# Two-operand products of a hybrid backbone moved to DVE, two gate blocks behind phase A's last step, and the modulation's matmuls placed among the attentions' projections

## The chip, the cores and the metric

One core of one Trainium2 chip runs the whole program. The metric is device time in microseconds (us) of one launch, as the median over several runs. Engines are named as in the profile: PE (TensorE matmuls), PEld (PE's weight loads), DVE (VectorE), ACT (ScalarE), POOL (GpSimd), SP (SyncE, which here only issues transfers).

## The reference

Two layers of a hybrid block work on 1024 latent tokens and 256 context tokens of width 1024. Each layer normalises its input with a modulation (shift, scale, gate) computed from a condition vector, projects it, and runs four mixers on columns of the projection: a Hyena long convolution, a bidirectional RWKV-7, a windowed attention and a dense attention with rotary positions. Each mixer's output is multiplied by its SiLU gate; the four are joined and projected back into the residual stream.

```python
def two_sided_fftconv(u, h_fwd, h_bwd, bias):
    L = u.shape[1]
    k = jnp.concatenate([h_fwd, jnp.zeros_like(h_fwd[:1]), h_bwd[:0:-1]], axis=0)
    U = jnp.fft.rfft(u, n=2 * L, axis=1)
    K = jnp.fft.rfft(k, n=2 * L, axis=0)
    y = jnp.fft.irfft(U * K[None], n=2 * L, axis=1)[:, :L]
    return y + u * bias

def hyena_branch(z, ...):
    v, x1, x2 = jnp.split(zc, 3, axis=-1)
    y = x1 * two_sided_fftconv(v, h[:, 0, 0], h[:, 0, 1], bias[0])
    return x2 * two_sided_fftconv(y, h[:, 1, 0], h[:, 1, 1], bias[1])

def rwkv7_scan(...):          # per token, both directions
    sa = jnp.einsum('bhvk,bhk->bhv', S, -kk_t)
    S = S * w_t + sa[..., None] * (kk_t * a_t)[:, :, None, :] + v_t[..., None] * k_t[:, :, None, :]
```

The RWKV state is not stepped token by token in the kernel: each tile of 128 tokens is brought into a form in which a triangular system of 32x32 blocks is solved.

## The kernel before

Matmuls at full precision are made of rounded parts: an operand is split into a high part (`wh`, written by ACT) and the rest (`wl = wr - wh`, L233), and three products are added up: `hhi` with `wh`, `hlo` with `wh`, `hhi` with `wl`. `chan` (L235) does this for a block of 128 projection columns; its output is transposed, so it runs in groups of 512, 512 and (for the context) 256 tokens, each 3 x 8 matmuls into one `acc`. 42 of the 58 blocks go through `chan`, 16 through `attn` (L297), which projects by tiles of 128 tokens.

A layer goes through these stages. Times are those of layer 0 in the profiled execution.

- Normalisation and the first filters of the Hyena (`hy_filters`), up to 133 us.
- `rw` (RWKV's convolutions), the context's filters and the first blocks of `first`, to 267.
- `modulation` (L116 to L152): the shift, scale and gate vectors from the condition. A load `mw` of 128x1024 (512 KB, L127, on SP's queue, three buffers) feeds two matmuls of 512 columns into `mps` (L130). Layer 0 does here its own gate and all of layer 1's: 32 loads, 64 such matmuls (the trace has four records for each load, as each runs in two passes). To 340.
- `attn`: the attentions' projections, with norms and rotary positions; q and k are stored as `qk_d`. To 476.
- Phase A (`phase_a`): ten tiles of 128 tokens go through `stage_a`, which makes the RWKV's decays, keys and the masked products `GG` (L591 to L598); beside it run Hyena's convolutions and the first gate blocks. Then the triangular systems are solved (L630 to L652) in 31 steps of a product `tmp` and a subtraction on `X`; here POOL takes two columns of each step and DVE the others. The last solve ends with a copy `XR` (L651) at 767; the stretch 729 to 774 is called the tail below.
- The Hyena (`hyena`), to 931: transposes `pd` (L1380), a transform of two streams by `pr` matmuls (L1396) and butterflies (`Dft.pair`, `Dft.odd`, `Dft.even`, `Dft.eight`), the product with the filter `Kf` (L1409, L1410, each cut into one half on DVE and one on POOL), the sums L1411 and L1412, and the way back (`pi`, L1441). Four such iterations follow one another in a layer. Its `u` lies in room that the last solve gives back. Beside it run six gate blocks (`beside`, the SiLU gates g = 1, 2, 3 of two blocks each; L274 and L275).
- `phase_b`, the attentions and the output projection, to 1458. Layer 1 follows in the same way to 2657 without a modulation and without context outputs.

The order on each engine is set by a list scheduler which simulates the program and gives each engine its instructions in the order of estimated readiness. Engines then run theirs strictly in that order and wait on semaphores. `nc.any` lets the scheduler choose the engine. `issue_after` (through `k.behind`) ties a matmul behind a given PE instruction; `k.spread` spreads blocks over the marks, which are PE instructions of the stage beside.

Of the kernel before, what the change touches and what calls it, by code (L numbers as in the profile page):

```python
# [170 lines left out]
def norm_in(k, hp, ap):  # L171
# [5 lines left out]
    with ExitStack() as es:  # L177
# [27 lines left out]
        for (t0, n), at, raw in zip(groups, ((hp, "lo8"),) + room, raws):  # L205
            i = 0 if t0 < 8 else 1
            low = lo[t0 * 128] = part(at, n, F32R, "hlo")
            for kc in range(8):
# [7 lines left out]
class Proj:  # L216
# [206 lines left out]
class Rwkv:  # L423
# [1235 lines left out]
```

## Time and profile before

| what | value |
| --- | --- |
| three runs | 2659.18, 2665.2, 2669.92 us; median 2665.2 |
| the profiled execution | 2658.42 us; span 2656.6, the granted clock 0.904 of full |
| PE busy | 2263.1 us (85%) |
| PEld busy | 1855.2 us (70%) |
| DVE busy | 1740.2 us (66%) |
| ACT busy | 1090.8 us (41%) |
| POOL busy | 1021.2 us (38%) |

The span is the time from the first to the last instruction of the profiled execution; 1.8 us lie around it. Busy shares say little about one stage, so the windows view, which cuts the span into stages, is the one to begin with.

### The profile page before, as it was taken

Reading aid. Unit: us, or ns where it says so; the run is one execution under the profiler, and the core shown is the slowest. Engines: PE = TensorE matmul, PEld = TensorE weight load, DVE = VectorE, ACT = ScalarE, POOL = GpSimd, SP = SyncE. Lnnn points to the kernel's source line nnn. Section 1 sums busy time; section 2 is a strip of 40 time slices with the busy share of each in tenths; the row PEclk is TensorE's granted clock in tenths of the full one; section 3 lists DMA queues with packets and bytes.
Section 4 is the critical chain, followed back from the end, with each engine's and each line's share of the span. In section 5 each row is a group of like instructions: output and inputs, shape, how many; then the busy total and the mean of one; then the engine's idle time right before and its main releaser. Section 6 shows DMA issues by size and latency. Waiting matters only on the chain. (4 is left out here: it accounts for less than half of the span.)

```text
span 2656.6 us, 45224 instructions
## 1 busy us (share of the span) xinstructions
PE 2263.1 (85%) x16864; PEld 1855.2 (70%) x16864; DVE 1740.2 (66%) x3710; ACT 1090.8 (41%) x2581; POOL 1021.2 (38%) x1279
## 2 busy tenths in 40 slices
PE   7799599899736779999899898989893586999898
PEld 3688089687636658787677797977672475888666
DVE  5976047578767856557634686657876886656743
ACT  5422023454411047566744322335441104776651
POOL 1632014356656712111432243323655763111342
PEclk9899799898867889999999899989885787999999
DMA  7223743555341354743433322444554226473242
GB/s 255 99 80 109 250 127 108 150 160 164 121 145 60 118 185 130 215 155 99 139 107 111 103 87 107 124 134 134 150 167 145 77 74 187 155 209 120 92 155 98
DMA packets 288695, 359.11 MB, mean 135 GB/s; under 512 B 108007, under 2 KB 229910, under 8 KB 283100
## 3 DMA queue, kind: packets, MB, share of 16 engines
q1 hardware_dynamic: 261704, 261.60, 31.7%
q0 software_dynamic: 11232, 70.78, 7.8%
q10 hardware_dynamic: 15540, 23.84, 2.8%
q8 instruction: 133, 2.18, 0.3%
q14 instruction: 86, 0.70, 0.1%
HBM read 227.31 MB, written 128.84 MB: 134 GB/s over the span
## 5 line engine op out<-in xcount | busy, mean ns | idle before, releaser
L233 POOL TENSOR_TENSOR wl<-wr,wh 128x1024 fp32r<-128x1024 f32 x58 | 149.3, 2579 | 290.0 <-ACT wh L232 243.7
L246 PE MATMUL acc<-hhi,wh 128*128 128x512 f32 (+1 forms) x896 | 221.2, 385 | 13.8 <-ACT wh L232 8.9
L985 DVE TENSOR_REDUCE st<-S 128x1 f32<-128x512 f32 (+1 forms) x320 | 172.6, 558 | 85.1 <-PE S L981 52.0
L246 PE MATMUL acc<-hlo,wh 128*128 128x512 f32 (+1 forms) x896 | 218.8, 378 | 2.6 <-DVE hlo L212 2.6
L246 PE MATMUL acc<-hhi,wl 128*128 128x512 f32 (+1 forms) x896 | 213.3, 375 | 0.0
L995 ACT ACTIVATE P<-S,st 128x512 f32<-128x512 f32 (+1 forms) x320 | 184.6, 587 | 39.8 <-DVE st L988 23.9
L246 PEld LDWEIGHTS acc<-hhi,wh 128*128 128x128 f32 x896 | 159.3, 198 | 45.6 <-ACT wh L232 10.8
L246 PEld LDWEIGHTS acc<-hlo,wh 128*128 128x128 f32 x896 | 157.8, 195 | 32.3 <-issue 4.5
L246 PEld LDWEIGHTS acc<-hhi,wl 128*128 128x128 f32 x896 | 157.9, 195 | 28.2 <-issue 3.0
L1011 PE MATMUL pt<-ident,P 128*128 128x128 f32 x976 | 160.5, 284 | 13.4 <-ACT P L995 7.1
L980 PE MATMUL S<-kp,qs 128*128 128x256 f32 (+2 forms) x384 | 143.4, 381 | 27.0 <-ACT P L995 18.3
L951 ACT COPY PT<-pt 128x512 f32<-128x512 f32 (+2 forms) x265 | 129.0, 506 | 49.1 <-PE pt L1011 46.7
L1011 PEld LDWEIGHTS pt<-ident,P 128*128 128x128 f32 x976 | 111.0, 142 | 44.6 <-issue 12.7
L1021 PE MATMUL O<-PT,V 128*64 128x256 f32 x976 | 138.4, 391 | 3.0 <-ACT PT L951 3.0
L981 PE MATMUL S<-kp,qs 128*128 128x256 f32 (+2 forms) x384 | 121.1, 326 | 3.6 <-DMA kp<-qk_d 3.6
L980 PEld LDWEIGHTS S<-kp,qs 128*128 128x128 f32 x384 | 75.8, 197 | 48.3 <-ACT P L995 28.1
L232 ACT ACTIVATE wh<-wr 128x1024 fp32r<-128x1024 f32 x58 | 60.7, 1057 | 110.7 <-PE acc L246 89.9
L1021 PEld LDWEIGHTS O<-PT,V 128*64 128x64 f32 x976 | 72.5, 138 | 45.1 <-issue 6.7
L337 PE MATMUL acc<-wh,hhi 128*128 128x256 f32 x608 | 93.4, 296 | 2.6 <-ACT wh L232 2.6
L337 PE MATMUL acc<-wl,hhi 128*128 128x256 f32 x608 | 88.5, 287 | 5.0 <-POOL wl L233 5.0
L258 ACT COPY zp<-acc 128x512 f32<-128x512 f32 (+1 forms) x64 | 33.7, 531 | 139.8 <-PE acc L246 80.1
L591 PEld LDWEIGHTS p_g<-AR,BKT 64*128 64x128 f32 x640 | 74.7, 218 | 23.2 <-DVE GG L598 5.5
(402 smaller groups left out, 5944.4 us busy)
## 6 DMA issues: line engine op xcount, KB each, us to landing
IN<-in_d POOLq DMA_DIRECT2D x18, 2048.0 KB, 9.4
wr<-in_w_in POOLq DMA_DIRECT2D x58, 512.0 KB, 4.2
mw<-in_mod_w SPq DMA_DIRECT2D x48, 512.0 KB, 4.6
in_d<-BK SPq DMA_DIRECT2D x20, 512.0 KB, 2.6
in_d<-AL SPq DMA_DIRECT2D x20, 512.0 KB, 2.7
kp<-qk_d SPq DMA_DIRECT2D x32, 320.0 KB, 7.8
qk_d<-qo SPq DMA_DIRECT2D x72, 128.0 KB, 1.9
in_d<-GG SPq DMA_DIRECT2D x18, 512.0 KB, 3.9
```

The source lines that it names most:

```text
L232: w.k.nc.scalar.activation(h, r, AF.Copy)
L233: w.k.nc.gpsimd.tensor_tensor(lw, r, h.bitcast(F32), op=ALU.subtract)
L246: nc.tensor.matmul(ps[:, :n], a[:, kc * 128:(kc + 1) * 128], b[:, kc, t0:t0 + n], start=(i == 0 and kc == 0), stop=(i == 2 and kc == 7))
L337: nc.tensor.matmul(ps[:, :256], x_[:, kc, t * 128:(t + 1) * 128], w_[:, kc, :], start=(n == 0 and kc == 0), stop=(n == 2 and kc == 7))
L591: nc.tensor.matmul(pg[:, hp, c], BKT[q, hp, c], AR[q, :, hp, half(c)], start=True, stop=True)
L951: nc.any.tensor_copy(o, i)
L980: nc.tensor.matmul(ps[:, w0:w0 + w], qs[:, hd % 2, hd // 2], kp[kv][0][:, t0:t0 + w], start=True, stop=False)
L981: nc.tensor.matmul(ps[:, w0:w0 + w], qs[:, hd % 2, hd // 2], kp[kv][1][:, t0:t0 + w], start=False, stop=not masks)
L985: TR(ng[:, i:i + 1], ps[:, :w0], axis=AX.X, op=ALU.max, negate=True)
L995: nc.scalar.activation(P[:, :w], ps[:, :w], AF.Exp, bias=gm, accum_out=den[:, i:i + 1])
L1011: nc.tensor.transpose(pt[:, i, :], P[:, i * 128:(i + 1) * 128], k.ident)
L1021: nc.tensor.matmul(O[kv * 64:kv * 64 + 64, 0], V[:, t, kv * 64:kv * 64 + 64], PTs[kv][:, i], start=(i == 0), stop=(i == nt - 1))
```

## The change

There are three parts.

The first: nearly every operation of POOL on two operands in SBUF goes to DVE. In all, POOL's instructions go from 1284 to 409, DVE's from 3712 to 4148; PE's 12744 and SP's 962 stay. Where DVE and POOL shared a step (the solve's columns, the product with `Kf`) one DVE instruction on the whole width takes its place. Where ACT copied from PSUM and POOL multiplied (`GG` of odd parity, `om` in the attention), one DVE product reads PSUM. Of the 58 splits `wl`, 42 (those of `chan`) go to DVE; the 16 of `attn` stay. Copies of `PV` and `ST` go to `nc.any`.

The second: the two blocks of gate 1 are tied behind the last mark of phase A (`end`), where before all six blocks were spread over the Hyena's matmuls; the other four still are.

The third: the modulation of layer 0 is written after 18 steps of `attn`'s generator instead of ahead of it, with its pool on the other side of SBUF.

The lines below are the diff's core. Left out are the same replacement of `PT` or `nc.gpsimd` by DVE in `operands`, `stage_a` (`ss`, `bs`), `Dft.even`, `Dft.eight`, the filters, the output projection's `wol`, and the context's Hyena.

```diff
-    def split(w, r, h, lw):
+    def split(w, r, h, lw, eng):
         w.k.nc.scalar.activation(h, r, AF.Copy)
-        w.k.nc.gpsimd.tensor_tensor(lw, r, h.bitcast(F32), op=ALU.subtract)
+        eng.tensor_tensor(lw, r, h.bitcast(F32), op=ALU.subtract)
...
-        w.split(r, h, lw)
+        w.split(r, h, lw, nc.vector)
...
-        pace = w.k.spread([x[1] for x in w.GR[-n:]] * len(todo), *part) if part else []
-        w.k.marks = []
+        if isinstance(part, tuple):
+            pace = w.k.spread([x[1] for x in w.GR[-n:]] * len(todo), *part)
+            w.k.marks = []
+        else:
+            pace = [part] * (n * len(todo)) if part else []
...
-                    e = TT
-                    if par:
-                        nc.scalar.activation(o, s, AF.Copy)
-                        s, e = o, PT
-                    e(o, s, gmask[:, d, :z].unsqueeze(1).to_broadcast([128, 4, z, 64]), op=ALU.mult)
+                    TT(o, s, gmask[:, d, :z].unsqueeze(1).to_broadcast([128, 4, z, 64]), op=ALU.mult)
...
-            PC = 2
-            tmp2 = sp.tile([128, 31 * PC], F32, tag="tmp2", bufs=1, name="tmp2")
             for j in range(31):
-                a, q = 31 - j, j + 1
-                c = min(q, PC)
-                for e, m, s, z in ((nc.gpsimd, tmp2, 0, c), (eng, tmp, c, q)):
-                    if z > s:
-                        n = z - s
-                        t = m[:P, 0:a * n].rearrange("p (q a) -> p q a", q=n)
-                        e.tensor_tensor(t, Lx[:P, j:j + 1, j + 1:].to_broadcast([P, n, a]), X[:, s:z, j:j + 1].to_broadcast([P, n, a]), op=ALU.mult)
-                        e.tensor_tensor(X[:, s:z, j + 1:], X[:, s:z, j + 1:], t, op=ALU.add)
+                a, n = 31 - j, j + 1
+                t = tmp[:P, 0:a * n].rearrange("p (q a) -> p q a", q=n)
+                TT(t, Lx[:P, j:j + 1, j + 1:].to_broadcast([P, n, a]), X[:, :n, j:j + 1].to_broadcast([P, n, a]), op=ALU.mult)
+                TT(X[:, :n, j + 1:], X[:, :n, j + 1:], t, op=ALU.add)
...
-        nc.scalar.activation(o, O[:, 1], AF.Copy)
-        nc.gpsimd.tensor_tensor(o, o, gt[:, :, t0:t0 + 128], op=ALU.mult)
+        nc.vector.tensor_tensor(o, O[:, 1], gt[:, :, t0:t0 + 128], op=ALU.mult)
...
-        h = R // 2
-        for a, z, e in ((h, R, TT), (0, h, PT)):
-            s = slice(a, z)
-            e(t[:, s], W[:, s], Kf[:, s, 1:2, :].to_broadcast([p, z - a, 2, 128]), op=ALU.mult)
-            e(W[:, s], W[:, s], Kf[:, s, 0:1, :].to_broadcast([p, z - a, 2, 128]), op=ALU.mult)
-            e(W[:, s, 0], W[:, s, 0], t[:, s, 1], op=ALU.subtract)
-            e(W[:, s, 1], W[:, s, 1], t[:, s, 0], op=ALU.add)
+        TT(t, W, Kf[:, :, 1:2, :].to_broadcast([p, R, 2, 128]), op=ALU.mult)
+        TT(W, W, Kf[:, :, 0:1, :].to_broadcast([p, R, 2, 128]), op=ALU.mult)
+        TT(W[:, :, 0], W[:, :, 0], t[:, :, 1], op=ALU.subtract)
+        TT(W[:, :, 1], W[:, :, 1], t[:, :, 0], op=ALU.add)
...
-                    if not last:
-                        for a, parts in ((l, (1,)), (l + 1, (0, 1))):
-                            with k.pool(f"mod{a}") as rs, k.pool(f"modp{a}", 1, PSUM) as rp:
-                                modulation(k, a, parts, 3, rs, rp)
                     with k.pool(f"pa{l}") as sa, k.pool(f"pap{l}", 1, PSUM) as pq:
-                        run(w.attn(sa, pq))
+                        at = w.attn(sa, pq)
+                        for _ in range(18):
+                            next(at)
+                        if not last:
+                            for a, parts in ((l, (1,)), (l + 1, (0, 1))):
+                                with tc.using_default_side(LEFT), k.pool(f"mod{a}") as rs, k.pool(f"modp{a}", 1, PSUM) as rp:
+                                    modulation(k, a, parts, 3, rs, rp)
+                        run(at)
...
                         run(rw.phase_a(re, rs, rp))
+                    end = k.marks[-1][1]
...
-                    w.beside([(g, i) for g in (1, 2, 3) for i in range(2)], PACE_H)
+                    w.beside([(1, i) for i in range(2)], end)
+                    w.beside([(g, i) for g in (2, 3) for i in range(2)], PACE_H)
```

How the order on the engines moves is shown at three places. First PE around the modulation of layer 0, in the kernel before. `mps` are the modulation's matmuls, `acc<-hhi,wh` those of the convolutions' blocks, `pk` those of the context's filters, and `acc<-wh_2240,hhi` the projections'.

```order
L246 MATMUL acc<-hhi,wl 128x512 x8
L1501 MATMUL pk<-sm,F 128x256 x2
...
L130 MATMUL mps<-mw,scc 2x512 x48
L145 MATMUL mpt<-ident,mr 128x128 x4
L130 MATMUL mps<-mw,scc 2x512 x16
L337 MATMUL acc<-wh_2240,hhi 128x256 x24
L337 MATMUL acc<-wl_2241,hhi 128x256 x8
```

And the same engine after: the end of the filters and the projections' first group, and a later place in the projections.

```order
L130 MATMUL mps<-mw,scc 2x512 x4
L1489 MATMUL pk<-sm,F 128x256 x2
L1489 MATMUL pk<-H,F 128x256 x2
...
L130 MATMUL mps<-mw,scc 2x512 x8
L340 MATMUL acc<-wh_2060,hhi 128x256 x24
L130 MATMUL mps<-mw,scc 2x512 x4
L340 MATMUL acc<-wl_2061,hhi 128x256 x8
...
L313 MATMUL qpt<-ident,qq 128x128
L130 MATMUL mps<-mw,scc 2x512 x6
L340 MATMUL acc<-wh_2468,hhi 128x256 x8
L340 MATMUL acc<-wl_2469,hhi 128x256 x8
```

One block of 64 matmuls, broken only by four transposes, has become pieces of two to eight, from the context's filters into the second half of the projections. Of the 32 loads 14 stand ahead of the second group of tiles of the projections, 18 behind.

Second, PE at the end of phase A in layer 0, before and after. `p_g` and `p_r` are phase A's last products, `pd` and `pr` the Hyena's first.

```order
L591 MATMUL p_g<-AR,BKT 128x128 x16
L620 MATMUL p_r<-VV,GG 64x64 x16
L1380 MATMUL pd<-ident,zc 128x128 x32
L1396 MATMUL pr<-u,F 128x128 x8
L246 MATMUL acc<-hhi,wh 128x512 x2
L1396 MATMUL pr<-u,F 128x128 x8
L246 MATMUL acc<-hhi,wh 128x512 x6
```

```order
L594 MATMUL p_g<-AR,BKT 128x128 x16
L619 MATMUL p_r<-VV,GG 64x64 x16
L246 MATMUL acc<-hhi,wh 128x256 x8
L246 MATMUL acc<-hlo,wh 128x256 x8
L246 MATMUL acc<-hhi,wl 128x256 x8
...
L246 MATMUL acc<-hhi,wl 128x256 x8
L1371 MATMUL pd<-ident,zc 128x128 x32
L1387 MATMUL pr<-u,F 128x128 x4
```

Seven groups of 24 matmuls, three of 256 columns and four of 512, now stand between the last `p_r` and the first `pd`. In layer 1 there are four, all of 512.

Third, DVE in an iteration of the Hyena in layer 0, before and after. `Z<-W,Kf` is the product with the filter, `gt<-gt,acc` a gate block's product.

```order
L1229 SCALAR_TENSOR_TENSOR G<-s_7009,s_6978 128x512
L1230 SCALAR_TENSOR_TENSOR G<-s_7009,s_6978 128x512
L1233 TENSOR_TENSOR W<-G 128x2x2x128
L1234 TENSOR_TENSOR W<-G 128x2x256
L275 SCALAR_TENSOR_TENSOR gt<-gt,acc 128x512
L1409 TENSOR_TENSOR Z<-W,Kf 128x1024
L275 SCALAR_TENSOR_TENSOR gt<-gt,acc 128x256
L1410 TENSOR_TENSOR W<-W,Kf 128x1024
L1411 TENSOR_TENSOR W<-W,Z 128x4x128
L1412 TENSOR_TENSOR W<-W,Z 128x4x128
```

```order
L1214 TENSOR_TENSOR W<-s_6811 128x2x128
L1215 TENSOR_TENSOR W<-s_6811 128x256
L275 SCALAR_TENSOR_TENSOR gt<-gt,acc 128x512
L1224 TENSOR_TENSOR W<-G 128x2x2x128
L1225 TENSOR_TENSOR W<-G 128x2x256
L1397 TENSOR_TENSOR Z<-W,Kf 128x2048
L233 TENSOR_TENSOR wl<-wr,wh 128x1024
L275 SCALAR_TENSOR_TENSOR gt<-gt,acc 128x512
L1398 TENSOR_TENSOR W<-W,Kf 128x2048
L1399 TENSOR_TENSOR W<-W,Z 128x8x128
L1400 TENSOR_TENSOR W<-W,Z 128x8x128
```

The two products and sums have twice their width, `Dft.even`'s operations (L1212 to L1215 after) and a split `wl` stand in DVE's row too.

## Rows read from the trace of the kernel before

**Rows 1.** Windows: busy time (instructions) of each engine by stage; then clock, DMA share, GB/s.

```profile
0.00:133.00 133.00, 95.87 (x463) 64.18 (x464) 104.48 (x144) 60.88 (x103) 55.93 (x55) 0.90 0.52 177
...
266.60:339.60 73.00, 41.18 (x133) 4.27 (x133) 2.69 (x9) 4.31 (x6) 5.91 (x8) 0.79 0.73 250
339.60:476.00 136.40, 135.28 (x1084) 133.37 (x1083) 81.01 (x314) 42.00 (x110) 44.88 (x36) 0.99 0.37 110
476.00:729.00 253.00, 225.32 (x1499) 182.12 (x1497) 194.29 (x343) 120.18 (x236) 143.17 (x216) 0.86 0.51 151
...
774.40:931.50 157.10, 113.73 (x624) 100.38 (x622) 133.97 (x128) 16.85 (x27) 110.85 (x72) 0.84 0.27 89
...
2059.00:2215.30 156.30, 100.95 (x518) 87.89 (x516) 134.81 (x125) 14.34 (x21) 109.77 (x72) 0.79 0.31 95
```

**Rows 2.** Timeline of PE in the modulation: start, length, instruction, idle before and releaser.

```profile
266.60 2.74 PE L130 MATMUL mps<-mw,scc 128*2 128x512 f32 x12 [0.68 <-ACT sets L1502]
...
311.24 1.03 PE L130 MATMUL mps<-mw,scc 128*2 128x512 f32 x4 [1.36 <-DMA mw<-in_mod_w]
```

**Rows 3.** Timeline of DVE in the Hyena of layer 1.

```profile
2059.15 0.69 DVE L1215 TENSOR_TENSOR s<-s,pr 128x512 f32<-128x512 f32 x1 [6.21 <-PE pr L1396]
2059.75 0.68 DVE L1217 TENSOR_TENSOR s<-s,pr 128x512 f32<-128x512 f32 x1
2060.47 0.42 DVE L1240 TENSOR_TENSOR s<-s 128x256 f32<-128x256 f32 x1
2060.81 0.42 DVE L1241 TENSOR_TENSOR s<-s 128x256 f32<-128x256 f32 x1
...
2062.62 2.81 DVE L1243 TENSOR_TENSOR s<-s 128x512 f32<-128x512 f32 x1
...
2087.99 0.69 DVE L1243 TENSOR_TENSOR s<-s 128x512 f32<-128x512 f32 x1 [1.15 <-POOL s L1417]
...
2095.51 0.69 DVE L1215 TENSOR_TENSOR s<-s,pr 128x512 f32<-128x512 f32 x1 [1.07 <-PE pr L1396]
```

**Rows 4.** Timeline of POOL in the same stretch.

```profile
2062.49 2.40 POOL L1429 TENSOR_TENSOR zc<-zc 128x1024 f32<-128x1024 f32 x1 [10.27 <-DMA zc<-hy_d]
```

**Rows 5.** Groups by line: count | busy us, mean ns of one | idle before.

```profile
L1409 DVE TENSOR_TENSOR Z<-W,Kf 128x1024 f32<-128x1024 f32 x8 | 25.4, 3178 | 0.2
```

**Rows 6.** Timeline of DVE in the first filters.

```profile
74.38 1.23 DVE L1321 TENSOR_TENSOR sm<-H 128x1024 f32<-128x1024 f32 x1
75.53 2.75 DVE L210 TENSOR_SCALAR raw<-raw,gs,sh 128x256 f32<-128x256 f32 x2
```

**Rows 7.** Timeline of PE at the tail and the beginning of the Hyena, layer 0.

```profile
727.85 0.91 PE L620 MATMUL p_r<-VV,GG 64*64 64x64 f32 x12 [2.93 <-POOL GG L598]
...
768.02 3.68 PE L1380 MATMUL pd<-ident,zc 128*128 128x128 f32 x16 [15.79 <-ACT u L1381]
...
779.63 1.98 PE L246 MATMUL acc<-hhi,wl 128*128 128x512 f32 x8
781.44 1.12 PE L246 MATMUL acc<-hhi,wh 128*128 128x256 f32 x8
782.39 1.12 PE L246 MATMUL acc<-hlo,wh 128*128 128x256 f32 x8
```

**Rows 8.** Timeline of DVE, the end of the last solve, layer 0.

```profile
766.25 0.68 DVE L651 COPY XR<-X 32x1024 f32<-32x1024 f32 x1 [1.34 <-POOL X L649]
```

**Rows 9.** Groups by line: the mask product of `GG`.

```profile
L598 POOL TENSOR_TENSOR GG<-GG,gmask 128x512 f32<-128x512 f32 x36 | 48.2, 1341 | 12.2 <-ACT GG L596 12.1
...
L598 DVE TENSOR_TENSOR GG<-p_g,gmask 128x512 f32<-128x512 f32 x36 | 24.6, 684 | 14.1 <-PE p_g L591 14.1
```

**Rows 10.** The page's groups, and who waited for PE's `acc` (us, times).

```profile
L233 POOL TENSOR_TENSOR wl<-wr,wh 128x1024 fp32r<-128x1024 f32 x58 | 149.3, 2579 | 290.0 <-ACT wh L232 243.7
...
L232 ACT ACTIVATE wh<-wr 128x1024 fp32r<-128x1024 f32 x58 | 60.7, 1057 | 110.7 <-PE acc L246 89.9
...
  ACT wh L232: 89.9, 28
```

More of the change, by code (lines that the diff above doesn't have):

```diff
@@ L328, in attn @@
                     r3 = r.rearrange("p (k c) -> p k c", k=8)
-                    w.split(r3, wh[:, :, b * 128:(b + 1) * 128], wl[:, :, b * 128:(b + 1) * 128])
+                    w.split(r3, wh[:, :, b * 128:(b + 1) * 128], wl[:, :, b * 128:(b + 1) * 128], nc.gpsimd)
                 H = 4 if half == 0 else 2
@@ L510, in stage_a @@
             nc.any.tensor_copy(ss[0], sig)
-            PT(ss[1], sig, ss[0].bitcast(F32), op=ALU.subtract)
+            TT(ss[1], sig, ss[0].bitcast(F32), op=ALU.subtract)
             E = []
@@ L560, in stage_a @@
                 bs = w1("bs")
-                PT(bs, kd[:, 0, :], kd[:, 1, :], op=ALU.add)
-                PT(bs, bs, r_, op=ALU.mult)
-                PT(bs, bs, rv[:, 2, :], op=ALU.mult)
+                TT(bs, kd[:, 0, :], kd[:, 1, :], op=ALU.add)
+                TT(bs, bs, r_, op=ALU.mult)
+                TT(bs, bs, rv[:, 2, :], op=ALU.mult)
                 nc.vector.tensor_reduce(w.bon[:, b, :], h4(bs), axis=AX.X, op=ALU.add)
@@ L725, in stage_b @@
                 for c in range(2):
-                    nc.gpsimd.tensor_copy(pv[half(1 - c), c], VS[half(1 - c)].rearrange("p (h v) -> p h v", h=4))
+                    nc.any.tensor_copy(pv[half(1 - c), c], VS[half(1 - c)].rearrange("p (h v) -> p h v", h=4))
                 PV.append(pv)
             if need_y:
-                nc.gpsimd.tensor_copy(ST[:, 1792:2048], VV[:, 0, :])
+                nc.any.tensor_copy(ST[:, 1792:2048], VV[:, 0, :])
             cols = lambda x: x.rearrange("p a (h e) -> p h a e", h=4)
@@ L1220, in even @@
         o = out.rearrange("p s j e -> p (s j) e")
-        s.PT(out[:, 0], AB[:, 0], AB[:, 1], op=ALU.add)
-        s.PT(out[:, 1], AB[:, 0], AB[:, 1], op=ALU.subtract)
-        s.PT(o[:, 4:8:3], A1, B1[:, ::-1], op=ALU.add)
-        s.PT(o[:, 5:7], A1[:, ::-1], B1, op=ALU.subtract)
+        s.TT(out[:, 0], AB[:, 0], AB[:, 1], op=ALU.add)
+        s.TT(out[:, 1], AB[:, 0], AB[:, 1], op=ALU.subtract)
+        s.TT(o[:, 4:8:3], A1, B1[:, ::-1], op=ALU.add)
+        s.TT(o[:, 5:7], A1[:, ::-1], B1, op=ALU.subtract)
     def odd(s, out, TU, CD):
@@ L1243, in eight @@
         s.TT(AB, S[:, 0::2], S[:, 1::2], op=ALU.add)
-        s.PT(AB1, S[:, 0::2], S[:, 1::2], op=ALU.subtract)
+        s.TT(AB1, S[:, 0::2], S[:, 1::2], op=ALU.subtract)
         s.even(out, AB, AB1[:, 0], AB1[:, 1])
@@ L1292, in hy_filters @@
     nc, A = k.nc, k.A
-    TT, PT = nc.vector.tensor_tensor, nc.gpsimd.tensor_tensor
+    TT = nc.vector.tensor_tensor
     R, p = R8, 128
@@ L1321, in hy_filters @@
             TT(sm, H[:, 0], H[:, 1], op=ALU.add)
-            PT(H[:, 1], H[:, 0], H[:, 1], op=ALU.subtract)
+            TT(H[:, 1], H[:, 0], H[:, 1], op=ALU.subtract)
             pm = (sm, H[:, 1])
@@ L1361, in hyena @@
     nc, A = k.nc, k.A
-    TT, PT = nc.vector.tensor_tensor, nc.gpsimd.tensor_tensor
+    TT = nc.vector.tensor_tensor
     n, p, R = L, 128, R8
@@ L1416, in forward @@
         TT(D[:, 0:2], W[:, 0:4:2], W[:, 1:4:2], op=ALU.subtract)
-        PT(S[:, 0:2], W[:, 0:4:2], W[:, 1:4:2], op=ALU.add)
-        PT(S[:, 2:4], W[:, 4:6], W[:, 6:8], op=ALU.add)
+        TT(S[:, 0:2], W[:, 0:4:2], W[:, 1:4:2], op=ALU.add)
+        TT(S[:, 2:4], W[:, 4:6], W[:, 6:8], op=ALU.add)
         ft.eight(Z, S, D, True)
@@ L1428, in inverse @@
             nc.sync.dma_start(out=gx[:, 1], in_=zd[:, 2, hf, 0:n])
-            PT(gx[:, 0], gx[:, 0], gx[:, 1], op=ALU.mult)
+            TT(gx[:, 0], gx[:, 0], gx[:, 1], op=ALU.mult)
             gv = gx[:, 0].rearrange("q (t r) -> q r t", r=R)
@@ L1463, in ctx_filters @@
     nc, A = k.nc, k.A
-    TT, PT = nc.vector.tensor_tensor, nc.gpsimd.tensor_tensor
+    TT = nc.vector.tensor_tensor
     bank = lambda nm: pp.tile([128, 512], F32, tag="b", bufs=3, name=nm)
@@ L1490, in ctx_filters @@
         TT(sm, H[:, 0], H[:, 1], op=ALU.add)
-        PT(H[:, 1], H[:, 0], H[:, 1], op=ALU.subtract)
+        TT(H[:, 1], H[:, 0], H[:, 1], op=ALU.subtract)
         pm = (sm, H[:, 1])
@@ L1509, in ctx_hyena @@
     nc, A = k.nc, k.A
-    TT, PT = nc.vector.tensor_tensor, nc.gpsimd.tensor_tensor
+    TT = nc.vector.tensor_tensor
     bank = lambda nm: pp.tile([128, 512], F32, tag="b", bufs=3, name=nm)
@@ L1521, in ctx_hyena @@
     gx = load(tile_("gx", [2, C]), k.gt_d[0:256, L:TOK].rearrange("(h p) t -> p h t", p=128))
-    PT(gx, gx, zc[:, 2], op=ALU.mult)
+    TT(gx, gx, zc[:, 2], op=ALU.mult)
     ux = []
@@ L1543, in ctx_hyena @@
             TT(Z[:, m, 0], Z[:, m, 0], t[:, 1], op=ALU.subtract)
-            PT(Z[:, m, 1], Z[:, m, 1], t[:, 0], op=ALU.add)
+            TT(Z[:, m, 1], Z[:, m, 1], t[:, 0], op=ALU.add)
         mj = [(m, j) for m in range(2) for j in range(2)]
@@ L1574, in program @@
     run = lambda g: [None for _ in g]
-    R = "right"
+    LEFT, R = "left", "right"
     with k.pool("cp", 1) as cp, k.pool("dp", 1, DRAM) as dp:
```

5 lines of the change are left out of this document (2 added, 3 removed).

## The prediction

> **What bounds the kernel now.** I read the busy time by stage first, because the whole-span shares mix stages with different limits. Six of its rows stand in [rows 1]. In the reader's place I would look for stages whose PE column is close to their length, and those whose PE column is not. The attentions' projections keep PE busy for 135.28 us of 136.40: there only PE work counts. Four other stretches leave PE idle.
>
> - The modulation, 73.00 us long: PE has 41.18 us, DVE 2.69, ACT 4.31, POOL 5.91. Nothing but transfers (250 GB/s) and the small matmuls is there. The PE timeline shows how it goes: four records of 1.03 us per load, each after an idle gap that ends with the arrival of `mw` [rows 2].
> - The hyena, 157.10 us in layer 0 and 156.30 in layer 1: DVE 133.97 and 134.81, POOL 110.85 and 109.77, PE 113.73 and 100.95 [rows 1]. DVE and POOL are both near full, and both are slowed: the next view, one iteration on DVE and POOL [rows 3, 4], has the same addition of 128x512 (L1243) at 2.81 us while POOL multiplies `zc`, and at 0.69 us 25 us later.
> - Phase A, 253.00 us in layer 0: PE 225.32 at a granted clock of 0.86, DVE 194.29, POOL 143.17 [rows 1]. No engine is full; the chain through the tiles is the limit.
> - The solve's tail before the hyena: PE stops at 728.8 (727.85 + 0.91) and works on the hyena's second stream only at 768.02 [rows 7].
>
> **The change part by part.**
>
> *The hyena's products on DVE.* The row that matters is the product of 1024 columns: 3178 ns mean on DVE while POOL works on the other half [rows 5]. The same width alone, with POOL quiet, takes 1.23 us, and the next instruction starts after 75.53 − 74.38 = 1.15 [rows 6]. So a half costs 2.6 times its price alone, which is more than one engine needs for both (2.30). The Trainium skill has this on the page "SBUF — State Buffer", section "Who interferes with whom": a DVE operation with two SBUF operands and a GpSimd operation that reads SBUF use one read port, under a lock. The trace agrees by the three rows just named.
>
> The price of a DVE instruction in a row is start to start: 0.60 us for 128x512 (2059.75 − 2059.15) and 0.34 for 128x256 (2060.81 − 2060.47) [rows 3], 1.15 for 128x1024 [rows 6]. A 2048-column one isn't in the trace; two of 1024 bound it from above at 2.30, and the slope (0.55 per 512 columns) gives 2.25, which I take. One iteration (two streams joined, two transforms) then is on DVE alone: 20 of 512 columns = 12.0; 12 of 256 = 4.1; 2 of 1024 = 2.3; 2 of 2048 = 4.5; 2 of 512 for `u` = 1.2. Sum 24.1 us. Add about 2.5 for gate blocks that fall in (a `wl` of 1.15 and two gates of 0.60) and 2 for the turn through PE: 28.5. The iteration before takes 2095.51 − 2059.15 = 36.4 us [rows 3]. Four iterations and 6 us of beginning and end: 120 against 157.1 and 156.3, that is −37 per layer. Bounds: nothing gained, if the chain and not the load is the limit, and at best 24.1 × 4 + 6 = 102, −55.
>
> *The two early gate blocks.* Behind phase A's last step stand seven groups in layer 0, before the transposes `pd`. By the hyena's rows a group of 512 is 3 × 1.83 = 5.5 us (from 779.63 to 781.44 for eight) and one of 256 is 3 × 0.95 = 2.9 [rows 7]: 4 × 5.5 + 3 × 2.9 = 30.7 us on PE. The hole there is 768.02 − 728.76 = 39.3 us. It covers them, with 3.7 for the first `pd` set now behind them, by 5 us. That hides them and takes 31 us of PE from the hyena. On DVE they put a `wl` of 1.15, four gates of 0.60 or less and waits into the last solve, which ended with `XR` at 766.25 [rows 8]; the solve's own steps lose their waits for POOL (1.34 us at the end). I charge 7 us of tail per layer: 3.6 for these instructions, 3.7 for the `pd` set when it ends up last. Bounds 0 and 15. Hyena and tail: −30 per layer, −60 in all; the ends are −110 and +30.
>
> *The modulation amid the projections.* 32 loads of 512 KB took 73.00 us, 2.28 each, of which 1.03 is PE [rows 1, 2]. In the changed order 14 loads are used before the second group of tiles of the projections and 18 later. For the first 14 I take 25 us: between 14.4 (all had arrived) and 32 (all paced by the transfers as before), nearer the upper, since they stand in the convolutions' last rows and there are few matmuls between. The other 18 cost PE 18.5, in a stage where PE is full [rows 1]. 73.0 − 25 − 18.5 = −30. Bounds: 0 if every load is waited for as before, since PE goes in order and a late `mw` stops the projections; −44 if all stands hidden with PE at 0.91 us per load (2.74 us for 12 would be the best run of them). SP, which issues the loads, now holds them between stores of `qk_d`; a full pool makes SP wait there and delays stores, whose readers come only in the attentions.
>
> *Phase A.* POOL's work goes to DVE at about half the price: the mask product of the 128x512 `GG` is 1341 ns on POOL and 684 on DVE, 36 each [rows 9], and ACT's copy ahead of it goes. Each chain becomes shorter: the two waits of `p_r` for `GG` go. But the load grows: 194.29 + 143.17 / 2 = 265.9 us of DVE in 253.00 if nothing of 194.29 was contention. With the products freed (a third of it by the hyena's ratio) it is nearer to 220. I take −10 for both layers; bounds −40 (the 28 us of PE idle in layer 0 gone and part of layer 1's) and +30 (13 us each, and a little).
>
> *Filters, convolutions, output projection, attentions.* At the start DVE has 104.48 of 133.00 and POOL 55.93 [rows 1], so 104.48 + 28 fills the stage without contention relief; elsewhere PE bounds. The 42 moved `wl` splits cost POOL 2579 ns each, and 1.15 on DVE [rows 10, 6]; POOL waited 243.7 us for `wh` ahead of them [rows 10], which was free on POOL and is not on DVE. I take −8; bounds −25 and +25. Attention: the copy on ACT and product on POOL become one DVE product beside PE's work: 0, ±10.
>
> **Sum.** −60 − 30 − 10 − 8 = −108. On the profiled execution, 2658.42 us, that is 2550. The median of the runs shown is 2665.2, 6.8 above it, so 2557 on the runs' scale; I take 2556.
>
> **The rivals.**
>
> *DVE becomes the bound outside the hyena.* What speaks for it is the 265.9 above, and the full start. Then phase A costs +13 per layer, the start +10, and the hyena and modulation still give 30 and 60 less 20 for a hyena bound by its chain: 2665 + 36 − 70 = 2631. Against it is the 3178 ns row: the relief is on DVE too. The Trainium skill's page "Perfetto Trace Analysis", section "Optimizing Scalar/DVE Operations", says that a saturated DVE may be relieved by offloading to Scalar or even GPSIMD, with the warning that the shared port may make this useless: by its first half this rival, by the second the forecast. The trace shows the load in [rows 1] and the lock in [rows 5].
>
> *The modulation gains nothing.* The loads are paced by the transfers wherever they stand, and PE waits in order. Speaks for it: each gap in [rows 2] ends with `mw`. Against: PE has 135.28 us of other matmuls beside them [rows 1]. 2556 + 30 = 2586.
>
> *The split in DVE's queue, the slower side.* ACT writes `wh` after waiting for PE's `acc`: 89.9 us over 28 waits, 3.2 each [rows 10]. The `wl` product stood on POOL, where such a wait held up nobody; on DVE all behind it waits, and PE waits for that. 42 splits × (3.2 + 1.15) = 183 us if all of them stop the critical work. Between none and all, the change turns from gain to loss when 108 / 4.35 = 25 of the 42 do. At 32, the time is 2665 − 108 + 139 = 2696. Against: the scheduler places the splits by its own estimate of their readiness, and the convolutions have slack on DVE (two `wl` buffers).
>
> *The halves were not slowed by each other.* Then the hyena's 2048-column products cost 2 × 3.2 and DVE alone is slower than both: per iteration about 24.1 + 8 = 32, plus turns 36: hyena at 0, and 2556 + 60 = 2616. Against it are rows 5 and 6 together.
>
> **Chances and range.** Forecast (sum within 35 us) 0.55; modulation gains nothing 0.15; DVE bound elsewhere 0.13; halves not slowed by each other 0.05; the split in the queue 0.05; a gain larger than 143 us, all bounds at their good ends, 0.07. What this kernel's measurement can tell from no change is 0.5%, 13 us. The forecast's own range is 2521 to 2591; with the rivals, 2505 to 2630 holds 8 in 10. Faster by over 0.5%: 0.89. Within: 0.05. Slower: 0.06.
>
> **What would show it.** Hyena: the `Z<-W,Kf` product at 128x2048 near 2.3 us, iterations of 28 to 30 us, no POOL in that stage. If that product is above 4 us, the reading of rows 5 and 6 is wrong. Tail: 30 us of `acc` matmuls in the old hole, and `XR` no later. Modulation: no stretch of `mps` alone longer than 30 us; if the projections' stage has idle on PE that ends with `mw`, the second rival is right. Phase A: DVE below 225 us; over 245, with PE idle ending with DVE, the first. Splits: DVE idle that ends with ACT's `wh` over 40 us in sum is the third. Above 2640 the forecast has failed altogether.

## The result, and the profile after

The changed kernel took 2538.16 us (median of 4 runs, 2534.96 to 2539.31), the kernel before 2662.19 beside it. The ratio is 0.9536, 95% interval 0.9498 to 0.9574: faster by 4.6%, 124 us. The forecast was 2556. The profiled execution has a span of 2537.5 us against 2656.6, so 119.1 us have to be found in the two traces.

The page's first lines come first. Read them beside the table of before: DVE's busy time is the same to 1 us (1740.2 before) with 436 more instructions, while POOL's fell from 1021.2 to 270.0.

```profile
PE 2231.6 (88%) x16864; PEld 1844.7 (73%) x16864; DVE 1740.8 (69%) x4146; ACT 1079.7 (43%) x2564; POOL 270.0 (11%) x404
```

The windows of after by stage (columns as in [rows 1]) answer to [rows 1]: the remainder of the modulation's loads ahead of the projections; the projections; phase A; the tail; the Hyena; in layer 1 the Hyena alone.

```profile
243.40:277.40 34.00, 23.52 (x88) 9.65 (x87) 13.85 (x19) 6.20 (x8) 5.89 (x8) 0.85 0.69 245
277.40:429.50 152.10, 151.36 (x1153) 133.29 (x1152) 77.74 (x322) 43.49 (x113) 36.09 (x34) 0.99 0.52 163
429.50:664.40 234.90, 211.77 (x1468) 172.33 (x1466) 194.41 (x410) 106.35 (x209) 14.72 (x28) 0.89 0.56 165
664.40:724.20 59.80, 40.47 (x227) 36.23 (x226) 37.93 (x104) 12.30 (x21) 1.12 (x2) 0.81 0.56 184
724.20:849.10 124.90, 88.86 (x503) 79.93 (x502) 110.83 (x176) 12.17 (x20) 0.00 (x0) 0.84 0.32 97
...
1968.20:2094.60 126.40, 76.90 (x420) 68.52 (x419) 109.36 (x172) 10.41 (x16) 0.00 (x0) 0.78 0.35 99
```

In phase A, DVE is busy for 194.41 us with 67 instructions more than before, where it was 194.29 in a longer stage [rows 1]. In the Hyena POOL does nothing, and DVE's busy time fell from 133.97 to 110.83 although it now does both halves (and 11 gate products where 16 stood). The stages, cut at the same instructions in both traces (last `p_r` of phase A, last `XR`, first and last work of the Hyena, and so on), give this balance, in us:

| stage | before | after | difference | forecast |
| --- | --- | --- | --- | --- |
| start to the projections' end, layer 0 | 471.9 | 428.9 | -43.0 | -38 (modulation -30, and the -8 for all filters and splits) |
| phase A, both layers | 501.5 | 460.5 | -41.0 | -10 |
| last `p_r` to last `XR` | 38.2, 39.4 | 51.6, 43.7 | +13.4, +4.3 | +14 |
| last `XR` to the Hyena's first sum | 7.5, 6.2 | 8.2, 7.2 | +1.7 | - |
| the Hyena | 157.1, 156.3 | 124.9, 126.4 | -32.2, -29.9 | -74 |
| phase_b, attentions, output projection, layer 0 | 527.7 | 533.9 | +6.2 | 0 |
| all else of layer 1 | | | +1.4 | 0 |

DVE in an iteration of the Hyena in layer 0 answers to [rows 3]: `Z<-W,Kf` is now the whole product of 2048 columns, and the additions that had cost 2.81 us beside POOL stand at 0.69.

```profile
752.85 0.69 DVE L1206 TENSOR_TENSOR s<-s,pr 128x512 f32<-128x512 f32 x1 [1.42 <-PE pr L1387]
...
758.52 0.69 DVE L1234 TENSOR_TENSOR s<-s 128x512 f32<-128x512 f32 x1
...
763.92 2.29 DVE L1397 TENSOR_TENSOR Z<-W,Kf 128x2048 f32<-128x2048 f32 x1
...
783.13 0.69 DVE L1206 TENSOR_TENSOR s<-s,pr 128x512 f32<-128x512 f32 x1 [1.86 <-PE pr L1387]
```

The iteration takes 783.13 − 752.85 = 30.3 us. Between these rows DVE idles only for 0.65, 0.50 and 1.86 us, each time for PE's `pi` or `pr`: the Hyena is now bound by DVE.

PE in the modulation answers to [rows 2]. Before the projections' second group of tiles the loads still come in bursts; later, beside two bursts of three, single loads stand 1.7 to 3.5 us apart among the projections, and PE waits for one of them once.

```profile
243.39 2.74 PE L130 MATMUL mps<-mw,scc 128*2 128x512 f32 x12
...
275.58 1.88 PE L130 MATMUL mps<-mw,scc 128*2 128x512 f32 x4 [4.82 <-DMA mw<-in_mod_w]
281.87 1.04 PE L130 MATMUL mps<-mw,scc 128*2 128x512 f32 x8
...
348.97 1.03 PE L130 MATMUL mps<-mw,scc 128*2 128x512 f32 x4
352.02 1.03 PE L130 MATMUL mps<-mw,scc 128*2 128x512 f32 x4
354.36 1.03 PE L130 MATMUL mps<-mw,scc 128*2 128x512 f32 x4
357.81 1.03 PE L130 MATMUL mps<-mw,scc 128*2 128x512 f32 x4 [0.74 <-DMA mw<-in_mod_w]
```

The tail in layer 0 answers to [rows 7, 8]: DVE's copies around the last two solves, then PE.

```profile
677.62 0.69 DVE L644 COPY XR<-X 64x1024 f32<-64x1024 f32 x1
...
689.18 0.68 DVE L634 COPY Lx<-Ld 32x1024 f32<-32x1024 f32 x1 [6.18 <-DMA Ld<-ls_d]
...
715.31 0.68 DVE L644 COPY XR<-X 32x1024 f32<-32x1024 f32 x1
```

```profile
662.36 2.04 PE L619 MATMUL p_r<-VV,GG 64*64 64x64 f32 x32
664.33 2.07 PE L246 MATMUL acc<-hhi,wh 128*128 128x256 f32 x8
...
694.78 1.12 PE L246 MATMUL acc<-hhi,wl 128*128 128x256 f32 x8
695.74 1.96 PE L1371 MATMUL pd<-ident,zc 128*128 128x128 f32 x16
717.03 3.68 PE L1371 MATMUL pd<-ident,zc 128*128 128x128 f32 x16 [19.33 <-ACT u L1372]
```

The gate groups fill the hole from 664.33 to 695.74, 31.4 us. But the solve ahead of the last copies its `XR` only 13.2 us after the last `p_r` (677.62 − 664.40), and the last one waits for it. In the kernel before it was 5.9 us, by its row beside [rows 7], and from there to the copy `Lx` of the last solve 8.3 us against 11.6 now:

```profile
734.64 0.69 DVE L651 COPY XR<-X 64x1024 f32<-64x1024 f32 x1
...
742.96 0.68 DVE L635 COPY Lx<-Ld 32x1024 f32<-32x1024 f32 x1 [7.62 <-DMA Ld<-ls_d]
```

In the changed kernel two products of the early gate groups stand among the last steps of the solve ahead, and DVE waits for ACT before each:

```profile
668.80 0.42 DVE L275 SCALAR_TENSOR_TENSOR gt<-gt,acc 128x256 f32<-128x256 f32 x1 [1.05 <-ACT gt L274]
...
674.48 0.69 DVE L275 SCALAR_TENSOR_TENSOR gt<-gt,acc 128x512 f32<-128x512 f32 x1 [0.71 <-ACT gt L274]
```

In layer 1 the trace has five groups between the last `p_r` and the first `pd` (1917.21 to 1947.00), one more than counted above from the order.

### The profile page after: what moved, and what is told of

Same layout as the page of the kernel before. It is cut to its first block, busy times and chain, and to the rows that moved or that the text cites. A ratio compares the mean times of both kernels' runs of the same rounds, so it can differ in the third digit from the quotient of the medians.

```text
span 2537.5 us, 44541 instructions
## 1 busy us (share of the span) xinstructions
PE 2231.6 (88%) x16864; PEld 1844.7 (73%) x16864; DVE 1740.8 (69%) x4146; ACT 1079.7 (43%) x2564; POOL 270.0 (11%) x404
## 4 chain that ended last, share of the span: by engine, by line
PE 68%; DVE 11%; DMA 9%; ACT 5%; issue 5%; SPq 1%; POOL 0%; ACTq 0%; POOLq 0%; DVEq 0%
PE acc L246 20%; PE acc L340 9%; PE ops L1112 8%; PE O L1014 3%; PE pt L1004 3%; DMA st_d<-ST 2%; PE p_g L594 2%; PE pk L1326 2%; PE S L973 2%; ACT P L988 1%; PE pr L1387 1%; PE mps L130 1%; PE S L974 1%; PE ph L1302 1%; DVE tmp L641 1%
## 5 line engine op out<-in xcount | busy, mean ns | idle before, releaser
L246 PE MATMUL acc<-hhi,wh 128*128 128x512 f32 (+1 forms) x896 | 219.8, 383 | 7.8 <-ACT wh L232 5.2
L246 PE MATMUL acc<-hlo,wh 128*128 128x512 f32 (+1 forms) x896 | 213.7, 373 | 0.0
L246 PE MATMUL acc<-hhi,wl 128*128 128x512 f32 (+1 forms) x896 | 211.0, 371 | 1.5 <-DVE wl L233 1.5
L246 PEld LDWEIGHTS acc<-hhi,wh 128*128 128x128 f32 x896 | 159.0, 198 | 40.0 <-ACT wh L232 7.2
L246 PEld LDWEIGHTS acc<-hhi,wl 128*128 128x128 f32 x896 | 155.2, 190 | 32.6 <-issue 5.8
L246 PEld LDWEIGHTS acc<-hlo,wh 128*128 128x128 f32 x896 | 157.1, 193 | 28.0 <-issue 2.0
L1004 PEld LDWEIGHTS pt<-ident,P 128*128 128x128 f32 x976 | 113.4, 144 | 43.3 <-issue 15.2
L1014 PE MATMUL O<-PT,V 128*64 128x256 f32 x976 | 133.2, 386 | 1.8 <-ACT PT L944 1.8
L345 ACT ACTIVATE qx<-acc 128x256 f32<-128x256 f32 x76 | 29.2, 384 | 137.9 <-PE acc L340 136.7
```

What stands on the lines that cost most here:

```text
L246: nc.tensor.matmul(ps[:, :n], a[:, kc * 128:(kc + 1) * 128], b[:, kc, t0:t0 + n], start=(i == 0 and kc == 0), stop=(i == 2 and kc == 7))
L1004: nc.tensor.transpose(pt[:, i, :], P[:, i * 128:(i + 1) * 128], k.ident)
L1014: nc.tensor.matmul(O[kv * 64:kv * 64 + 64, 0], V[:, t, kv * 64:kv * 64 + 64], PTs[kv][:, i], start=(i == 0), stop=(i == nt - 1))
```

## The experiments

Each is timed against the kernel before on the same chip; times are medians. The edits are made to the changed kernel, except the last one. A loss or gain in us is a difference of medians to the changed kernel's 2538.16, which was not taken beside these runs, and is good to some us only: by the ratios to the kernel before, the first four come out 4 to 7 us lower.

**The modulation back ahead of the projections.**

```diff
+                    if not last:
+                        for a, parts in ((l, (1,)), (l + 1, (0, 1))):
+                            with k.pool(f"mod{a}") as rs, k.pool(f"modp{a}", 1, PSUM) as rp:
+                                modulation(k, a, parts, 3, rs, rp)
...
-                        at = w.attn(sa, pq)
-                        for _ in range(18):
-                            next(at)
...
+                        run(w.attn(sa, pq))
```

> The change with the modulation of layer 0 written ahead of the attentions' projections again; all else as changed. Theory (the loads' transfers now run beside the projections' matmuls): the bare stretch of about 70 us returns, the projections shrink from 152 to about 133, and the time is 2538 + 30 to 45 = 2568 to 2583. Rival (the stage became shorter because DVE's operations around it did): at most 2548.

2573.46 us, ratio 0.9645 (0.9624 to 0.9665): 35.3 us lost (29 by the ratios), and the bare stretch is back. Its window on the trace:

```profile
266.10:336.80 70.70, 40.54 (x133) 4.00 (x133) 1.96 (x8) 5.38 (x8) 8.04 (x5) 0.81 0.74 249
```

The projections are back at 129.2 us. The theory holds. The start without the moved loads is only 2.8 us shorter than in the kernel before (336.8 against 339.6), and the projections 3.1 (129.2 against 132.3). So of the -43.0 some 37 (466.0 − 428.9) belong to the modulation.

**All six gate blocks spread again.**

```diff
-                    w.beside([(1, i) for i in range(2)], end)
-                    w.beside([(g, i) for g in (2, 3) for i in range(2)], PACE_H)
+                    w.beside([(g, i) for g in (1, 2, 3) for i in range(2)], PACE_H)
```

> The change with all six gate blocks spread over the Hyena's matmuls again. Theory of the forecast (31 us of PE put into the old hole count in the Hyena): 2538 + 20 to 30 = 2558 to 2568. Rival (the Hyena is held by DVE, and what the gates put into the last solve and the Hyena loses there is alike): the tail is 5 to 14 us shorter in layer 0, the Hyena longer by as much, and the time 2530 to 2545.

2539.99 us, ratio 0.9519 (0.9497 to 0.9540): no difference that these runs can tell. The tail is 8.3 and 3.7 us shorter (43.3 and 40.0), phase A 2 and 8 us longer, the Hyena within 2 us. The rival holds for the Hyena, which got its PE work back and stayed within these 2 us: DVE bounds it. But the seven groups of layer 0 did not all come from there. The windows of PE's gate and convolution matmuls (L246) in phase A and in the Hyena of layer 0, before and after:

```profile
471.90:728.80 256.90, 106.49 (x437) 75.97 (x435) 0.86 0.51 151
774.40:931.50 157.10, 75.83 (x384) 63.40 (x382) 0.84 0.27 89
```

```profile
428.90:664.40 235.50, 87.79 (x390) 64.11 (x388) 0.89 0.56 165
724.20:849.10 124.90, 51.86 (x258) 43.38 (x258) 0.84 0.32 97
```

Some five groups of 24 left the Hyena, 24 us of PE, and two left phase A. In layer 1 it was four and one. By this run the move gives 10 us in the phases A and costs 12 in the tails.

**stage_a's products on POOL again.**

```diff
-            TT(ss[1], sig, ss[0].bitcast(F32), op=ALU.subtract)
+            PT(ss[1], sig, ss[0].bitcast(F32), op=ALU.subtract)
...
+                    e = TT
+                    if par:
+                        nc.scalar.activation(o, s, AF.Copy)
+                        s, e = o, PT
+                    e(o, s, gmask[:, d, :z].unsqueeze(1).to_broadcast([128, 4, z, 64]), op=ALU.mult)
```

(and the three `bs` products)

> The change with stage_a's products (ss, bs three times, GG of odd parity with ACT's copy) on POOL again. Theory (these products' price and the waits on POOL made phase A longer): phase A is 10 to 17 us longer in each layer, 2558 to 2573. Rival (phase A became shorter because of the splits or the solves): at most 2545. Forecast's own term: phase A worth 10 in both layers, 2548.

2563.28 us, ratio 0.9606 (0.9578 to 0.9635): 25 us lost (19 by the ratios), in phase A 6 and 12, in the tails 4 and 10. The theory holds in its sum; a part of its loss falls in the tail, where the solve ahead of the last copies its `XR` only 17.2 us after the last `p_r` (13.2 in the changed kernel).

**The Hyena's and the transforms' products on POOL again.**

```diff
-        TT(t, W, Kf[:, :, 1:2, :].to_broadcast([p, R, 2, 128]), op=ALU.mult)
...
+        for a, z, e in ((h, R, TT), (0, h, PT)):
...
-        s.TT(out[:, 0], AB[:, 0], AB[:, 1], op=ALU.add)
+        s.PT(out[:, 0], AB[:, 0], AB[:, 1], op=ALU.add)
```

(and the rest of `even`, `AB1`, `S`, `gx`)

> The change with the Hyena's and the transforms' products on POOL again (both halves, even, AB1, S, gx), splits and gates as changed. Theory (two-operand products on DVE and POOL hold each other up): the 1024-column product is back above 2.9 us on both, the Hyena takes 150 us or more, 2538 + 55 to 70 = 2593 to 2608. Rival (the Hyena became shorter because two gate blocks left it): at most 2560.

2584.52 us, ratio 0.9696 (0.9664 to 0.9728): 46 us lost, less than the 55 expected, and far above the rival; the Hyena takes 148.0 and 148.6 us, just short of the 150 expected. Half of the product's groups are back at their price, as in [rows 5]; the other half (the first product on POOL, the second on DVE) stand at 2715 and 2698 ns:

```profile
L1402 POOL TENSOR_TENSOR W<-W,Kf 128x1024 f32<-128x1024 f32 x8 | 25.5, 3186 | 0.5
L1401 DVE TENSOR_TENSOR Z<-W,Kf 128x1024 f32<-128x1024 f32 x8 | 25.3, 3164 | 0.2
```

**Only that product in halves again.**

```diff
-        TT(t, W, Kf[:, :, 1:2, :].to_broadcast([p, R, 2, 128]), op=ALU.mult)
-        TT(W, W, Kf[:, :, 0:1, :].to_broadcast([p, R, 2, 128]), op=ALU.mult)
+        h = R // 2
+        for a, z, e in ((h, R, TT), (0, h, PT)):
...
```

> The change with only the product with Kf, L1409 to L1412 of before, in halves on DVE and POOL again. Theory (any two-operand pair holds the other up, this one is 5 of some 14 us of POOL per iteration): an iteration is 1 to 3 us longer, 2538 + 8 to 24 = 2546 to 2562, with the 1024-column product near 3 us. Rival (this product is the whole of it): over 2575. Second rival (halves beside each other still save time): under 2535.

2550.30 us, ratio 0.9576 (0.9548 to 0.9604): 12 us lost, as the theory has it: the Hyena is 9.6 and 10.2 us longer, 2.5 us per iteration. The halves are quicker than the 3 us it named, DVE's above all:

```profile
L1400 POOL TENSOR_TENSOR Z<-W,Kf 128x1024 f32<-128x1024 f32 x8 | 22.7, 2837 | 207.4 <-DVE W L1215 207.4
L1400 DVE TENSOR_TENSOR Z<-W,Kf 128x1024 f32<-128x1024 f32 x8 | 19.2, 2404 | 0.1
```

DVE's half takes 2404 ns. The whole takes 2289 on DVE alone. Two engines here are slower than one.

**The 42 splits on POOL again.**

```diff
-        w.split(r, h, lw, nc.vector)
+        w.split(r, h, lw, nc.gpsimd)
```

> The change with the 42 splits wl of chan on POOL again. Theory (on DVE they cost 51 us of busy time and 18.7 us of waits, but lie beside PE's work; on POOL they take 2.4 us or more and slow DVE's two-operand operations): 2538 + 3 to 15 = 2541 to 2553. Rival (a wait for wh in DVE's order holds up what stands behind it, so that the forecast's slower side is there in small): 2515 to 2533.

2551.23 us, ratio 0.9577 (0.9549 to 0.9606): 13 us lost, and by the stages all of it in phase A (242.1 and 231.3 us against 235.5 and 225.0). POOL's `wl` row, and DVE's in the changed kernel, with what DVE waited for ahead of it:

```profile
L233 POOL TENSOR_TENSOR wl<-wr,wh 128x1024 fp32r<-128x1024 f32 x58 | 148.2, 2560 | 678.0 <-ACT wh L232 434.5 <-PE acc L246 111.0 <-issue 110.4
```

```profile
L233 DVE TENSOR_TENSOR wl<-wr,wh 128x1024 fp32r<-128x1024 f32 x42 | 51.1, 1219 | 18.7 <-PE acc L246 10.0 <-ACT wh L232 7.7 <-issue 0.8
```

So the split in DVE's order waits 18.7 us in all, not 42 × 3.2 = 134, and is a gain.

**Two columns of the solve on POOL again.**

```diff
+            PC = 2
+            tmp2 = sp.tile([128, 31 * PC], F32, tag="tmp2", bufs=1, name="tmp2")
...
+                for e, m, s, z in ((nc.gpsimd, tmp2, 0, c), (eng, tmp, c, q)):
```

> The change with two columns of each solve's step on POOL again. DVE spent 70 us in the solves of layer 0 with POOL's 61 beside it, and 67 without. Theory (POOL's share bought nothing): 2538 to 2546, the last solve as long as with DVE alone. Rival (the solve's DVE load is what made phase A and the tail late): the last solve 3 us shorter in each layer, phase A shorter, 2520 to 2532.

2530.75 us, ratio 0.9506 (0.9478 to 0.9533). The interval overlaps the changed kernel's; its four runs reach from 2529.91 to 2540.24. The stages do not bear either theory out: tails 5 us shorter in layer 0 and 3 longer in layer 1, phase A 1 shorter and 4 longer; what is gained, 12 us, is in the attentions and output projections. Inconclusive.

**Another buffer for the last solve.**

```diff
-            nc.sync.dma_start(out=X, in_=A["eye32"][:P])
+            nc.gpsimd.memset(X, 0.0)
+            nc.gpsimd.memset(X.rearrange("p a b -> p (a b)")[:, ::33], 1.0)
...
-            XR = sp.tile([128, 32, 32], F32, tag="Ld", bufs=1, name="XR")
+            XR = sp.tile([128, 32, 32], F32, tag="Lx", bufs=1, name="XR")
```

> The change, and in the solves the copy XR takes the buffer of Lx instead of that of Ld, so that Ld can be loaded before the solve ahead has ended; X is set to the identity by two memsets on POOL instead of a transfer. Theory (the last solve waits 11.5 us in layer 0 for stores and loads through buffers that the solve ahead holds): the tail is 5 to 9 us shorter in each layer, 2520 to 2530. Rival (something else is late then: PE's gate groups, the transposes' zc, the store of X): under 3 us in all, 2533 to 2541.

2525.16 us, ratio 0.9481 (0.9457 to 0.9504). The time is in the expected range, the place is not. The mechanism is there, in the copies around the solves of layer 0:

```profile
677.00 0.69 DVE L645 COPY XR<-X 64x1024 f32<-64x1024 f32 x1
682.28 0.95 DVE L634 COPY Lx<-Ld 32x1024 f32<-32x1024 f32 x1 [4.59 <-DMA ys_d<-XR]
```

From the one copy to the other it takes 5.3 us instead of 11.6. But the solve ahead now ends 17.9 us after the last `p_r`, as its order changed too, and phase A and tail together are 4.8 us shorter in layer 0 and 1.2 longer in layer 1. The attentions and the output projection of layer 0 gave 9.1. The edit changes `XR`'s buffer and the way `X` is set at once, so what each of them does is not shown.

**The changed kernel again.** No edit.

> The changed kernel itself once more, beside the next three on one chip, as the base for the version with the tail. 2535 to 2540. If it comes out within 5 us of the version with the tail's buffers, that one's gain was the chip's; if 10 us or more above it, the gain stands.

2534.11 us (2533.03 to 2537.29), ratio 0.9525 (0.9505 to 0.9546). The version with the tail's buffers is 9 us faster by the medians, on another chip, and between the two marks set (5 and 10 us); the intervals touch at 0.9504 and 0.9505: likely faster, by some 0.4%, but not settled.

**The tail's buffers and the solve's columns on POOL.** The last two edits together.

> The tail's buffers (XR in Lx, X by memset) and two columns of each solve's step on POOL again. Theory (both shorten the work that the last solve waits for, by different means: 13 us by the one, 7 by the other): 2512 to 2522. Rival (both times came from another order in the attentions, which either edit brings about): 2522 to 2534.

2527.42 us, ratio 0.9502 (0.9480 to 0.9523). The gains don't add, so the theory falls and the rival's range holds. Here phase A and tail of layer 0 are 9 us shorter than in the changed kernel (277.9 against 287.1), and the attentions with the output projection at 534.6, not at the 524.8 of the version before. Over all these kernels that stretch reaches from 524 to 542. Two executions of the changed kernel agree (533.9 and 534.6), so it seems to go with the program, not with the run; the order that the scheduler finds is the likely cause, and what in it makes the difference stays open.

**Only the products on DVE.** The modulation ahead and six gates spread, both as in the two edits above.

> Of the change only the products on DVE: the modulation ahead of the projections and six gates spread, as before. Theory (the parts add up: 35 for the modulation, 0 to 2 for the gates): 2538 + 36 = 2574, within 8. Rival (the modulation's placement needed a quiet DVE): over 2585.

2585.04 us, ratio 0.9712 (0.9687 to 0.9736): the products alone are worth 76 us, 11 fewer than the theory expected, and just what the rival set as its limit.

**Only the modulation moved, in the kernel before.**

```diff
-                        run(w.attn(sa, pq))
+                        at = w.attn(sa, pq)
+                        for _ in range(18):
+                            next(at)
...
+                        run(at)
```

> The kernel before with only the modulation moved among the projections. Theory (transfers beside matmuls; POOL and DVE have no part in it): 2665 - 35 = 2630, within 8. Rival (with the splits of the convolutions on POOL, loads and projections wait for it): over 2645.

2622.19 us, ratio 0.9853 (0.9830 to 0.9875): 39 us, without any product moved. The two parts alone make 76 + 39 = 115 of 127 (2660.86 − 2534.11). The other 12 would be the gates, but undoing them alone cost 2, and each of the three medians is good to 6 us. The attentions and output projection of layer 0 in the kernel with the products alone, 542 us against 534, make 8 of the difference. The rival of the run ahead (the placement needs a quiet DVE) is excluded as it was put: here it gains 39 us with DVE and POOL as before. By the stages a part of it is left. Up to the projections' end only 27.5 us are gained (471.9 − 444.4), against the 37 in the changed kernel; the other 12 stand in later stages, 8.7 of them in phase A. The early loads begin at 261.33 here and at 243.39 there, and the projections start 23.0 us after 266.60, where the modulation began before:

```profile
261.33 1.88 PE L130 MATMUL mps<-mw,scc 128*2 128x512 f32 x6
...
289.62 3.13 PE L337 MATMUL acc<-wh,hhi 128*128 128x256 f32 x24
```

## Why the prediction was right, point by point

*The modulation.* Forecast -30, measured 37 by its stages; by the whole times 29 to 35 when it is put back, 39 when it alone is moved. The 18 late loads cost 22.3 us against 18.5: the projections take 151.5 us with them and 129.2 in the run whose edit changes nothing else. The 14 early ones were mis-sized: 25 us were taken, and with the start 336.8 us long when the loads stand alone for 70.7, they cost 277.4 − (336.8 − 70.7) = 11.3. That is below even the bound of 14.4; the first of them stand at 243.39, amid the context's filters. In the kernel before with only the modulation moved they cost 23.0, near the 25. So the gain beyond the forecast came with the rest of the change, an interplay that the forecast did not have. The rival that each load would be waited for falls, by the view of PE's waits over the span (total, times, longest), before and after:

```profile
PE mps L130 <- DMA mw<-in_mod_w: 32.6, 23, 5.9
```

```profile
PE mps L130 <- DMA mw<-in_mod_w: 7.8, 6, 4.8
```

*The Hyena.* The prices were right: 2.29 us for the product against 2.25, and 30.3 us for the iteration against 28.5. The forecast had two gates and one `wl` in it; this iteration has three and one, and DVE waits 3.0 us for PE where 2 were taken. So -37 per layer became -32 and -30. The gates had less part in it than written: they took 24 us of PE from the Hyena of layer 0, not 31, and putting them back changed nothing there. That the halves did not slow each other is refuted by the run with the halves alone. (This rival was priced at 60 us; with the tail's 14 still lost it would have been 74.) The Trainium skill says on the page "SBUF — State Buffer", section "Who interferes with whom", that a DVE instruction with two SBUF inputs contends with a GpSimd instruction that reads SBUF. These rows agree: 2289 ns for the whole on DVE alone against 2404 for half of it beside POOL.

*The tail.* +14 forecast, +17.7 measured (13.4 + 4.3). The early gate groups are most of it, as forecast: with the gates spread again 8.3 and 3.7 us of it are gone. The way was another. The seven groups fitted the hole (31.4 us against 30.7), and the second `pd` set did not end up later by itself. In layer 0 the solve ahead of the last became late by 7.3 us (13.2 − 5.9), the copy `Lx` followed it 3.3 us later than before (11.6 − 8.3), and the last solve itself took 2.8 us more. With the gates spread the first of these is 9.1 us and not 13.2; so 4 of the 7.3 went with the gate groups. What makes the other 3 is open: with `stage_a`'s products back on POOL it is 17.2, so these products on DVE are not shown to be the cause; with the splits back on POOL it is 8.0. A late solve pushes the load of `Ld` and `X`, which share its buffers; the version with another buffer removed 6 us there.

*Phase A.* This is the step that was mis-sized: -10 forecast, -41.0 measured, just beyond the good bound of -40. I had put DVE at 220 us in layer 0 and had it near the bound. It stayed at 194.41. Of what POOL's products added, the freed ones gave much back, as one group shows, DVE's product `BK` of 64x512, before and after:

```profile
L556 DVE TENSOR_TENSOR BK<-kd,en 64x512 f32<-64x512 f32 x40 | 37.7, 943 | 1.3
```

```profile
L559 DVE TENSOR_TENSOR BK<-kd,en 64x512 f32<-64x512 f32 x40 | 27.4, 686 | 1.3
```

PE's waits for POOL's `GG`, 11.7 us in all before, became 4.6 for DVE's. In the phases A the run with these products back on POOL returned 17.6 of the 41 us, the run with the splits 13.0, the run with the gates spread 9.8. The last was not in the forecast, which took all seven groups from the Hyena: PE's busy time in phase A of layer 0 fell from 225.32 to 211.77 [rows 1], with two gate groups fewer and the granted clock at 0.89 for 0.86. These shares are rough, as an edit of the Hyena alone (the product in halves) also made the phases A 7.4 us longer.

*Splits.* The slower rival priced a wait at 3.2 us and asked for 25 of 42 to decide. They waited 18.7 us in all, 0.4 each, and 7.7 of it for `wh`; the forecast had named 40 as the sign of this rival.

*The rest.* -8 was expected in the filters and splits. 6 us came up to the projections' end (471.9 − 466.0), none in the same part of layer 1; the 13 that the splits are worth stand in phase A. The attentions of layer 0 became 6 us longer, within the ±10 given.

In the profiled executions the sum is 119 against 108: phase A's surplus of 31 and the start's of 5 outweigh what the Hyena lacked (12), the tail and its end (5), and the attentions and layer 1's rest (8). That the total came within 18 us is in part luck: the mechanisms of the modulation and the Hyena held, but single terms were off by up to 31 us and with opposite signs.

## What to carry to other kernels

Where DVE and POOL both work on two operands from SBUF, first compare one instruction's time beside the other engine with its time alone. If half the work beside it takes longer than the whole alone, as 2404 against 2289 ns here, the work belongs on one engine, and the load this adds may be nothing, since the other instructions get their time back. Freeing an engine that does not bound the stage (PE in the Hyena, 24 us in layer 0) bought nothing there, and its work was paid for where it went (the tail). An edit's worth should be looked up by stages, in the stages that it did not touch too.

## What the runs showed that was not expected

- DVE's busy time did not change (1740.2 and 1740.8 us) with 436 instructions more, while POOL lost 875 and its own busy time fell by 751 us.
- Small edits in the solve moved the attentions of layer 0, which they do not touch, by 9 us (534 and 525): that is as much as a real edit brings.
